# A two-layer hybrid trunk on one core: scan tables copied later and in two halves, and the first column tiles started after the last channel tile

## The chip, the cores and the metric

The kernel runs as one program on one core of a Trainium2 chip. The metric is device time in microseconds (us), from the start of the program to its end. The core has a matrix engine (PE, with its weight loads as PEld), a vector engine (DVE), a scalar engine (ACT), a general engine (POOL) and a sync engine (SP) that here only issues DMA transfers. They run at the same time, each through its own fixed list of instructions, and wait for each other through semaphores.

## What is computed

Two token groups (128 context tokens, 512 noisy tokens) go through the same two layers. Each layer, cut to what this case touches:

```python
sh1, sc1, g1, sh2, sc2, g2 = split(mod)          # mod = silu(c) @ w_ada + b_ada
u = x * (1.0 + sc1) + sh1                        # modulated input, D_MODEL = 1024
z = u @ p["w_in"]                                # the widest product: q, k, v, s_in, f_in, gates
ssm_y, ssm_state = _s5_bidirectional(s_in, ...)  # scan over time, both directions
ssm_y = gelu(ssm_y); ssm_y = ssm_y * sigmoid(ssm_y @ p["w_glu"] + p["b_glu"])
merged = g_a * (attn @ w_br_attn) + g_s * (ssm_y @ w_br_ssm) + g_f * (four @ w_br_four)
x = layer_norm(ALPHA * x + g1 * (merged @ p["w_out"]))
h = dwconv3((x * (1.0 + sc2) + sh2) @ p["w_up"]); ...; x = layer_norm(ALPHA * x + g2 * (... @ p["w_down"]))
```

The scan is a complex linear recurrence with per-state factors `lb` and input factors `f`. The kernel works it in blocks of eight time steps, for which it needs the powers of `lb` up to eight and `f` times those powers: these are the scan tables.

## The kernel before, in words

**Products.** Every large product is made in f32 out of three matmuls (L137 to L139): weights and activations are each split in a high part (`wh`, `uh`: a cast on ACT, L113) and a low part (`wl`, `ul`: what the cast lost, a subtraction on DVE, L115, or for some weights on POOL, L119). The weights of one column tile come by DMA as `wraw` (three buffers, issued by SP), are split, and serve both token halves: half 0 has 256 columns, half 1 has 384. `mm_wz` is the product with `w_in` (the code calls it wz).

**Start of layer 0.** `mod` is made in eight channel tiles dt = 0 to 7 (`ada_first`): a 1 MB block `ablk` arrives by DMA, is multiplied on PE (`adps`, L254), copied by ACT (`adar`, L257), transposed on PE (`adpt`, L259) and added up on DVE. After each channel tile `block(dt)` scales that part of x into `ut` (on ACT, L381, or on POOL, L379; two buffers for both halves) and splits it into `uh` and `ul`. Meanwhile the first four column tiles of half 0 are run piece by piece (`mm_first`, L1365): `WAT` says after which channel tile each begins. `MOD0` says which channel tiles are scaled on POOL. The operands of half 1 are made from dt = 5 on, between the others.

**Scan tables.** `ssm_scalars` makes the powers `PW` and the factors `FB` for both layers on DVE, in a scratch pool `zoh`. Eight copies on ACT, 64 x 512 elements each (L574 to L578), lay them out as `LT` and `FTab`.

**Preparation of the scan** (`ssm_prep`): eight chunks for layer 0, which DVE, DVE and POOL take in turn, later eight for layer 1, all on POOL. A chunk reads `bc` (by DMA, few buffers, so a load waits until PE has finished with an earlier chunk), multiplies it with `FTab` to `wbt` and with `LT` to `wct` (L647 to L649), and PE transposes `wbt` (`ptp`, copied by ACT to `wtt`) and multiplies `wct` (`pkp`). The results go to DRAM (`wbd`, `wcd`, `pd`) and come back as `wbs`, `wcs`, `Ms`. DVE begins with the preparation of layer 0 when the last operands are split. In the same stretch `shift` adds the position shift to x on DVE (L405), out of two PSUM banks that `mm_wz` then needs.

**The scan of layer 0** (`ssm`): SP loads `U` (eight transfers of short rows out of `sd`), PE multiplies `wbs` with `U` (`psv`, L691), DVE scans (L707, L710), copies the states to `Hr` (L724 to L727), and PE makes the output (`psy`, L738 and L740), which ends in `Yh`, goes through DRAM and returns as the operand `gh` of the product with `w_glu`. These steps lie between the column tiles of `mm_wz`.

**Order.** A scheduler lays out each engine's list from the dependencies when the kernel is built, with its own estimate of durations; `behind(x)` and `issue_after` only say what may not stand ahead of x. Memory of a closed pool is given to later tiles: a tile in the place of `zoh` waits until `zoh` has been read for the last time.

## Time and profile before

| | before |
|---|---|
| time, median of 3 runs (lowest to highest) | 2274.53 us (2269.32 to 2278.03) |
| the profiled execution's own time | 2270.7 us |
| its span | 2268.9 us |
| mean granted TensorE clock | 0.987 of full speed |
| PE busy | 2192.8 us, 97% of the span |
| DVE, ACT, POOL busy | 66%, 39%, 28% of the span |

The span is what the trace covers; the time holds 1.8 us more. A busy PE can still run at half speed: the granted clock of a stretch tells that, and 0.5 of it is 1.2 GHz, 1.0 is 2.4 GHz. Times below are counted from the start of the span. Almost all that the change moves lies between 25 and 395 us, up to the first matmul of `w_glu`.

### The profile page before, as it was taken

The numbers are of one execution on the slowest core, as the hardware profiler recorded it, in microseconds if no ns is written. First come the engines' busy times: TensorE is split into PE (matmuls) and PEld (weight loads), VectorE is DVE, ScalarE is ACT, GpSimd is POOL, SyncE is SP. The second block draws the span as 40 slices with busy tenths as digits, with TensorE's granted clock in tenths as the row PEclk, the third lists the DMA queues.
The fourth block names the chain that finished last, engine by engine and source line by source line (L and its number), as shares of the span: only waits on it lengthen the run. The fifth ranks groups of instructions, "written<-read, shape, count | busy, mean of one in ns | idle before, by whom it ended". The sixth has DMA issues, their size and how long they took to land.

```text
span 2268.9 us, 40864 instructions
## 1 busy us (share of the span) xinstructions
PE 2192.8 (97%) x15696; PEld 2106.3 (93%) x15696; DVE 1488.4 (66%) x3646; ACT 880.5 (39%) x1799; POOL 626.9 (28%) x795
## 2 busy tenths in 40 slices
PE   6899999998999999999999999999999999999997
PEld 4899989898799999999999999999779999999997
DVE  7956751556647788998974277457755766465475
ACT  5343323344633532431434322334553543242243
POOL 0339952006465300100136000001536620110103
PEclk9999989999999999999999999999999999999998
DMA  7886665625042135445536735642204122222221
GB/s 276 219 260 214 204 190 188 207 86 183 1 127 84 62 107 167 143 146 171 158 91 175 179 128 149 179 140 85 70 5 151 57 84 66 84 75 65 84 75 47
DMA packets 172645, 294.00 MB, mean 130 GB/s; under 512 B 48129, under 2 KB 114081, under 8 KB 171425
## 3 DMA queue, kind: packets, MB, share of 16 engines
q1 hardware_dynamic: 171584, 291.12, 41.8%
q8 instruction: 124, 2.03, 0.4%
q14 instruction: 73, 0.59, 0.1%
q10 hardware_dynamic: 864, 0.26, 0.1%
HBM read 241.57 MB, written 49.75 MB: 128 GB/s over the span
## 4 chain that ended last, share of the span: by engine, by line
PE 83%; DVE 7%; DMA 3%; ACT 2%; issue 1%; SPq 1%; POOL 1%; POOLq 0%; DVEq 0%; ACTq 0%
PE mm_w_up L138 8%; PE mm_w_up L137 8%; PE mm_w_up L139 8%; PE mm_wz L137 6%; PE mm_wz L138 6%; PE mm_wz L139 6%; PE mm_w_down L139 4%; PE mm_w_down L137 4%; PE mm_w_down L138 4%; PE mm_qkv L1114 4%; PE mm_pv L1179 2%; PE mm_w_br L137 2%; PE mm_w_br L138 2%; PE mm_w_br L139 2%; PE pt L1232 2%; PE S L1221 2%
## 5 line engine op out<-in xcount | busy, mean ns | idle before, releaser
L113 ACT CAST wh<-wraw 128x1024 fp32r<-128x1024 f32 (+1 forms) x224 | 232.8, 1040 | 446.5 <-PE mm_w_down L138 118.2
L138 PE MATMUL mm_w_up<-ul,wh 128*128 128x256 f32 (+1 forms) x1280 | 393.9, 309 | 0.0
L139 PE MATMUL mm_w_up<-uh,wl 128*128 128x256 f32 (+1 forms) x1280 | 393.8, 309 | 0.0
L137 PE MATMUL mm_w_up<-uh,wh 128*128 128x256 f32 (+1 forms) x1280 | 391.9, 309 | 0.4 <-ACT wh L113 0.4
L119 POOL TENSOR_TENSOR wl<-wraw,wh 128x256 fp32r<-128x256 f32 x224 | 175.2, 814 | 711.8 <-ACT wh L113 710.6
L115 DVE TENSOR_TENSOR wl<-wraw,wh 128x1024 fp32r<-128x1024 f32 (+1 forms) x168 | 211.7, 1260 | 160.6 <-ACT wh L113 159.1
L137 PE MATMUL mm_wz<-uh,wh 128*128 128x384 f32 (+1 forms) x832 | 266.2, 321 | 7.3 <-ACT uh L113 4.0
L1258 DVE SCALAR_TENSOR_TENSOR acc<-mm_w_up,cw,acc 128x127 f32<-128x127 f32 (+2 forms) x616 | 229.0, 399 | 60.0 <-ACT acc L1264 32.3
L138 PE MATMUL mm_wz<-ul,wh 128*128 128x384 f32 (+1 forms) x832 | 262.3, 315 | 0.4 <-POOL ul L119 0.3
L139 PE MATMUL mm_wz<-uh,wl 128*128 128x384 f32 (+1 forms) x832 | 262.1, 315 | 0.0
L137 PEld LDWEIGHTS mm_w_up<-uh,wh 128*128 128x128 f32 x1280 | 242.0, 189 | 0.6 <-ACT wh L113 0.6
L139 PEld LDWEIGHTS mm_w_up<-uh,wl 128*128 128x128 f32 x1280 | 242.3, 189 | 0.2 <-POOL wl L119 0.2
L138 PEld LDWEIGHTS mm_w_up<-ul,wh 128*128 128x128 f32 x1280 | 242.2, 189 | 0.0
L139 PE MATMUL mm_w_down<-hh,wl 128*128 128x256 f32 (+1 forms) x632 | 195.1, 310 | 0.6 <-DVE wl L115 0.6
L138 PE MATMUL mm_w_down<-hh,wh 128*128 128x384 f32 (+1 forms) x632 | 195.5, 310 | 0.0
L137 PE MATMUL mm_w_down<-hh,wh 128*128 128x384 f32 (+1 forms) x632 | 193.5, 311 | 0.0
L137 PEld LDWEIGHTS mm_wz<-uh,wh 128*128 128x128 f32 x832 | 160.2, 193 | 16.5 <-issue 6.1
L138 PEld LDWEIGHTS mm_wz<-ul,wh 128*128 128x128 f32 x832 | 159.9, 192 | 2.0 <-issue 1.0
L139 PEld LDWEIGHTS mm_wz<-uh,wl 128*128 128x128 f32 x832 | 159.7, 192 | 0.7 <-issue 0.4
L289 DVE SCALAR_TENSOR_TENSOR adjunk<-araw,cb 128x512 f32<-128x512 f32 x192 | 138.3, 720 | 16.9 <-DMA araw<-in_w_ada_t_dram 14.1
L1264 ACT ACTIVATE acc<-mm_w_up,cw 128x384 f32<-128x384 f32 (+1 forms) x176 | 107.8, 614 | 62.5 <-PE mm_w_up L139 62.3
L139 PEld LDWEIGHTS mm_w_down<-hh,wl 128*128 128x128 f32 x632 | 119.1, 189 | 1.5 <-DVE wl L115 1.5
(464 smaller groups left out, 5212.4 us busy)
## 6 DMA issues: line engine op xcount, KB each, us to landing
wraw<-in_w_up_dram SPq DMA_DIRECT2D x88, 512.0 KB, 3.5
wraw<-in_wz_dram SPq DMA_DIRECT2D x64, 512.0 KB, 4.1
araw<-in_w_ada_t_dram SPq DMA_DIRECT2D x48, 512.0 KB, 3.8
araw<-in_w_ada_dram SPq DMA_DIRECT2D x32, 512.0 KB, 3.9
wraw<-in_w_down_dram SPq DMA_DIRECT2D x32, 512.0 KB, 3.5
wraw<-in_w_br_dram SPq DMA_DIRECT2D x24, 512.0 KB, 3.8
td<-gt SPq DMA_DIRECT2D x48, 192.0 KB, 1.9
tl<-td SPq DMA_DIRECT2D x48, 192.0 KB, 3.5
```

Source lines behind the costliest of these rows:

```text
L113: nc.scalar.copy(h, src)
L115: return nc.vector.tensor_tensor(l, src, h.bitcast(F32), OP.subtract)
L119: last = eng.tensor_tensor(l[:, w], src[:, w], h[:, w].bitcast(F32), OP.subtract)
L137: mm(ps, wh, xh, start=j == 0, stop=False)
L138: mm(ps, wh, xl, start=False, stop=False)
L139: mm(ps, wl, xh, start=False, stop=j == n - 1)
L289: nc.vector.scalar_tensor_tensor(junk[:, :k.stop - k.start], raw[:, d], 1.0, cb[v], OP.mult, OP.mult, accum_out=part[:, c, vec - a, dt + d ...
L1114: nc.tensor.matmul(ps[:, :256], lt, w[:, c0:c0 + 256], start=k == 0, stop=k == 23)
L1179: nc.tensor.matmul(po[64 * hh:64 * hh + 64, :256], vt[:, kt + 1, kv * 64:kv * 64 + 64], PT[hh][:, kt], start=kt == 0, stop=kt == 5, tile_p ...
L1221: nc.tensor.matmul(S[:, b, :384], q, kt[:, hl, P + b * 384:P + (b + 1) * 384], start=hl == 0, stop=hl == 1)
L1258: nc.vector.scalar_tensor_tensor(o, src, w, o, OP.mult, OP.add)
L1264: nc.scalar.activation(acc, ps, AF.Identity, bias=b, scale=w1)
```

## The change

The numbers `WAT` and `MOD0` change, the table copies leave `ssm_scalars` for a function of their own, and the operands of half 1 are all made after the last channel tile.

- `WAT` goes from (3, 6, 7, 7) to (3, 7, 7, 7): the second column tile also begins only after the last channel tile.
- `MOD0`: half 1 was scaled for dt = 1, 3, 5, 7 on POOL and else on ACT; now all eight are on POOL.
- Half 1 is split only after channel tile 7 and its matmuls have been written.
- `ssm_tables(l)` copies the half of the tables that layer l reads, in eight copies of 64 x 256 elements, `FTab` first, and negates its part of `LT` on DVE. The copies for layer 0 stand behind the last cast of half 1, those for layer 1 behind the last `wtt` copy of the preparation of layer 0.
- The scratch pool `zoh` stays open until the second table copies and is closed there.

```diff
@@ -53,8 +53,8 @@
 ART = "wraw"
 WB = 3
 XB = 5
-WAT = (3, 6, 7, 7)
-MOD0 = (((), ()), ((1, 3, 5, 7), ()))
+WAT = (3, 7, 7, 7)
+MOD0 = (((), ()), (range(8), ()))
 FS = 10
 MODS = (((1, 3, 5, 7), ()), ((), (1, 3, 5, 7)))
 
@@ -110,7 +110,7 @@
 
     def split(self, h, l, src, eng=None):
         nc = self.nc
-        nc.scalar.copy(h, src)
+        self.cast = nc.scalar.copy(h, src)
         if eng is None:
             return nc.vector.tensor_tensor(l, src, h.bitcast(F32), OP.subtract)
         n = l.shape[-1]
@@ -474,7 +474,10 @@
         self.LT = p.tile([P, 3, G, 8], F32, name="LT")
         self.FT = p.tile([P, 2, G, 8], F32, name="FTab")
         L8 = self.L8 = s.tile([P, 2, G, 2], F32, name="L8")
-        with tc.tile_pool(name="zoh", bufs=1) as z:
+        self.zoh = ExitStack()
+        if True:
+            z = self.zoh.enter_context(tc.tile_pool(name="zoh", bufs=1))
+
             def t(n):
                 return z.tile([P, G], F32, name=n)
             V = nc.vector
@@ -567,22 +570,29 @@
             V.tensor_tensor(f[:, 1, 0], acc, den, OP.mult)
             a = [f[:, ri].broadcast_to((P, 8, G)) for ri in range(2)]
             cmul(FB, 0, 8, a, [PW[:, ri, 0:8] for ri in range(2)], 8)
-            fw, bw = slice(0, 64), slice(64, 128)
-            for ri in range(2):
-                o = self.LT[:, ri].rearrange("p g t -> p t g")
-                cp = nc.scalar.copy
-                cp(o[fw], PW[fw, ri, 1:9])
-                cp(o[bw, ::-1], PW[bw, ri, 1:9])
-                o = self.FT[:, ri].rearrange("p g t -> p t g")
-                cp(o[fw, ::-1], FB[fw, ri])
-                cp(o[bw], FB[bw, ri])
-            V.tensor_scalar(self.LT[:, 2], self.LT[:, 1], -1.0, None, op0=OP.mult)
             V.tensor_copy(L8[:, 0, :, 0], PW[:, 0, 8])
             V.tensor_copy(L8[:, 0, :, 1], PW[:, 1, 8])
             V.tensor_scalar(L8[:, 1, :, 0], PW[:, 1, 8], -1.0, None, op0=OP.mult)
             V.tensor_copy(L8[:, 1, :, 1], PW[:, 0, 8])
             self.fzero = p.tile([P, 2, G], F32, name="fzero")
             V.tensor_copy(self.fzero, f[:, :, 0])
+            self.powers = PW, FB
+
+    def ssm_tables(self, l):
+
+        PW, FB = self.powers
+        cp = self.nc.scalar.copy
+        gs = slice(32 * l, 32 * l + 32)
+        fw, bw = slice(0, 64), slice(64, 128)
+        for ri in range(2):
+            o = self.FT[:, ri, gs].rearrange("p g t -> p t g")
+            cp(o[fw, ::-1], FB[fw, ri, :, gs])
+            cp(o[bw], FB[bw, ri, :, gs])
+        for ri in range(2):
+            o = self.LT[:, ri, gs].rearrange("p g t -> p t g")
+            cp(o[fw], PW[fw, ri, 1:9, gs])
+            cp(o[bw, ::-1], PW[bw, ri, 1:9, gs])
+        self.nc.vector.tensor_scalar(self.LT[:, 2, gs], self.LT[:, 1, gs], -1.0, None, op0=OP.mult)
 
     def ssm_open(self):
 
@@ -658,7 +668,7 @@
                 pt = zp.tile([P, 512], F32, name="ptp", tag="ptp", bufs=1)
                 for q in range(4):
                     nc.tensor.transpose(pt[:, q * P:(q + 1) * P], w[:, 2 * hh + q // 2, q % 2], self.ident)
-                nc.scalar.copy(wt[:, 2 * hh:2 * hh + 2], pt.rearrange("p (g r q) -> p g r q", g=2, r=2))
+                self.turned = nc.scalar.copy(wt[:, 2 * hh:2 * hh + 2], pt.rearrange("p (g r q) -> p g r q", g=2, r=2))
             self.ld(wb[ch], wt.rearrange("p g r q -> p (g r q)"))
             c = z.tile([P, 4, 2, P], F32, name="wct", tag="wct", bufs=2)
             prod(c, 0, (lr, nb(cr)), (li, nb(ci)), OP.subtract)
@@ -1345,13 +1355,9 @@
 
         def block(dt):
             nc.vector.tensor_scalar(sc[:, dt], self.mod[0][:, 1, dt], 1.0, None, op0=OP.add)
-            for half in range(2):
-                if half == 0 or dt > XB:
-                    ends[half] = self.modsplit(xs[half][:, dt], half, sc, sh, dt, self.u[half, "h"], self.u[half, "l"])
+            ends[0] = self.modsplit(xs[0][:, dt], 0, sc, sh, dt, self.u[0, "h"], self.u[0, "l"])
             if dt == XB:
                 self.ld(xs[1], self.i["xt"][:, :, HS[1]])
-                for d in range(dt + 1):
-                    ends[1] = self.modsplit(xs[1][:, d], 1, sc, sh, d, self.u[1, "h"], self.u[1, "l"])
             while len(tiles) < 4 and (WAT[len(tiles)] == dt):
                 src = ("wz", (0, len(tiles)))
                 self.first[src] = self.wunit(self.usrc(src))
@@ -1364,17 +1370,25 @@
                     for k, (a, b) in enumerate(((h, "h"), (h, "l"), (l, "h"))):
                         nc.tensor.matmul(ps, a[:, w], self.u[0, b][:, kt], start=kt == 0 and k == 0, stop=kt == KT - 1 and k == 2)
                 t[1] = dt + 1
+            if dt == KT - 1:
+                for d in range(KT):
+                    ends[1] = self.modsplit(xs[1][:, d], 1, sc, sh, d, self.u[1, "h"], self.u[1, "l"])
 
         with tc.tile_pool(name="first", bufs=1, side="right") as fp, tc.tile_pool(name="firstp", bufs=1, space=PSUM) as self.adp:
             self.adar = fp.tile([P, 256], F32, name="adar")
             self.ablk[0] = self.ada_block(fp, 0)
             self.ld(xs[0], self.i["xt"][:, :, HS[0]])
             self.ada_first(fp, block)
+        with self.behind(self.cast):
+            self.ssm_tables(0)
         self.pin = False
         self.pre = {j: t[0] for j, t in enumerate(tiles)}
         self.xd = [self.dram.tile([P, KT, NTOK], F32, name=f"xd{l}") for l in range(NL)]
         with self.behind(ends[0]), self.behind(ends[1]):
             self.ssm_prep(0, (0, 0, 1))
+            with self.behind(self.turned):
+                self.ssm_tables(1)
+            self.zoh.close()
             self.shift(xs, self.xd[0])
         for l in range(layers):
             self.layer(l)
```

In the lists of the engines the change shows at three places. The names are those of the sections above; `x2` is two equal instructions in a row, and a number behind a name tells two tiles apart.

**ACT at the start, before:** the eight table copies stand between the scalings (`ut`) and casts (`uh_260` of half 0) of the last channel tiles and ahead of the second weight cast (`wh`).

```order
L574 COPY LT<-PW 64x8x64
L575 COPY LT<-PW 64x8x64
L113 CAST uh_260<-ut 128x256
L577 COPY FTab<-FB 64x8x64
L578 COPY FTab<-FB 64x8x64
L381 ACTIVATE ut<-xs,mod_85,su_264 128x128 x2
L381 ACTIVATE ut<-xs,mod_85,su_264 128x384
L113 CAST wh<-wraw 128x1024
L113 CAST uh_260<-ut 128x256
L577 COPY FTab<-FB 64x8x64
L578 COPY FTab<-FB 64x8x64
L113 CAST uh_262<-ut 128x384
```

The same place after: the last casts of half 0 (`uh_250`), then those of half 1 (`uh_252`), and only then the tables, half as long.

```order
L113 CAST wh<-wraw 128x1024
L381 ACTIVATE ut<-xs,mod_85,su_254 128x128 x2
L113 CAST uh_250<-ut 128x256
L113 CAST uh_252<-ut 128x384 x3
L792 COPY sre<-mm_first 128x256
L113 CAST uh_252<-ut 128x384
L792 COPY sre<-mm_first 128x256 x2
L113 CAST uh_252<-ut 128x384 x4
L589 COPY FTab<-FB 64x8x32
L590 COPY FTab<-FB 64x8x32
```

Nothing of the tables is left between the casts of half 0, and no scaling of half 1 is on ACT any more; they are eight in a row on POOL.

**SP around the loads of U, before:** `U` is loaded while the preparation of layer 0 is under way.

```order
L103 DMA Ms<-pd_695 16x8x128 x2
L103 DMA bc<-in_ssm_bc_dram 128x256
L103 DMA pd_695<-ksb 128x144
L103 DMA Ms<-pd_695 16x8x128 x4
L103 DMA U<-sd_1302 16x32x80 x2
L103 DMA wcd_694<-wct 128x1024
L103 DMA U<-sd_1302 16x32x80 x6
L103 DMA Ms<-pd_695 16x8x128
L103 DMA wbd_693<-wtt 128x1024
```

After, `U` stands behind the last chunk of that preparation, with all that belongs to it in one row; the first of them waits for an ACT instruction, since `U` lies where `zoh` lay.

```order
L103 DMA wbd_692<-wtt 128x1024
L103 DMA U<-sd_1311 16x32x80 x5
L103 DMA pd_694<-ksb 128x144
L103 DMA U<-sd_1311 16x32x80 x3
L103 DMA wbs<-wbd_692 128x1024 x2
L103 DMA Ms<-pd_694 16x8x128 x16
L103 DMA wcd_2195<-wct 128x1024
L103 DMA bc<-in_ssm_bc_dram 128x256
L103 DMA td_1313<-gt 128x384
L103 DMA td_1313<-gt 128x256
L103 DMA wbs<-wbd_692 128x1024
```

What moved: eight loads of `U`, two of `wbs` and sixteen of `Ms` now stand in a row, and behind them the `bc` of the second chunk of layer 1, which was ahead of the first chunk's `wcd` before, and the next `wbs`.

**POOL behind that, after:** the first chunk of layer 1 ends with `wct_2237`, the second begins with `bc_2268`.

```order
L658 TENSOR_TENSOR pb_2242<-bc_2197,LT_105 128x512
L659 TENSOR_TENSOR wct_2237<-wct_2237,pb_2238 128x4x128
L659 TENSOR_TENSOR wct_2237<-wct_2237,pb_2242 128x4x128
L641 TENSOR_TENSOR pt1_2276<-fzero_247,bc_2268 128x64
L642 TENSOR_TENSOR bb_2272<-fzero_247,bc_2268 128x64 x2
L657 TENSOR_TENSOR wbt_2285<-bc_2268,FTab_106 128x4x128
```

The `wcd_2195` of SP stores `wct_2237`, and the load of `bc_2268` stands behind it, so that POOL's second chunk now waits for SP, and SP for POOL's first.

On PE the first `psv` goes from row 456 of the list to row 876, the first `psy` that reads `Hr` from 1384 to 1634 and the last `psy` from 1534 to 1779. The first matmul of `w_glu` is row 1958 in both, and from there to the end the lists are the same but for a few swaps.

## Rows read from the trace of the kernel before

**Rows 1.** The page's chain that ended last: share of the span by engine.

```profile
PE 83%; DVE 7%; DMA 3%; ACT 2%; issue 1%; SPq 1%; POOL 1%; POOLq 0%; DVEq 0%; ACTq 0%
```

**Rows 2.** PE's waits, 0 to 60 us: total, times, longest, in us.

```profile
PE mm_first L1365 <- ACT uh L113: 6.7, 2, 5.5
```

**Rows 3.** Groups by line and form, ACT, 24 to 62 us: busy, mean ns | idle before.

```profile
L381 ACT ACTIVATE ut<-xs,mod,su 128x384 f32<-128x384 f32 x4 | 2.8, 699 | 0.1
L578 ACT COPY FTab<-FB 64x512 f32<-64x512 f32 x2 | 2.3, 1138 | 0.0
```

**Rows 4.** SP's timeline, then DMA issues of 15 to 27 us with us to landing.

```profile
25.73 0.90 SPq L103 DMA_DIRECT2D wraw<-in_wz_dram  x2
...
wraw<-in_wz_dram SPq DMA_DIRECT2D x3, 512.0 KB, 12.0
```

**Rows 5.** Busy us (instructions) of PE, PEld, DVE, ACT, POOL; granted clock; then PE's timeline.

```profile
40.00:43.00 3.00, 2.75 (x13) 2.46 (x13) 1.53 (x3) 2.96 (x5) 0.67 (x1) 0.50 0.46 115
46.60:50.20 3.60, 3.60 (x33) 3.60 (x31) 2.91 (x14) 1.92 (x6) 1.06 (x1) 1.00 0.71 204
...
55.62 0.45 PE L137 MATMUL mm_wz<-uh,wh 128*128 128x384 f32 x1 [0.30 <-ACT sre L782]
```

**Rows 6.** POOL's and DVE's timeline: start, duration, idle before and its releaser.

```profile
43.85 0.67 POOL L379 TENSOR_SCALAR ut<-xs,su,mod 128x384 f32<-128x384 f32 x1 [1.94 <-DVE ul L115]
48.49 1.06 POOL L379 TENSOR_SCALAR ut<-xs,su,mod 128x384 f32<-128x384 f32 x1 [3.98 <-DVE mod L263]
...
54.67 0.19 DVE L623 TENSOR_SCALAR nci<-bc 128x64 f32<-128x64 f32 x1
```

**Rows 7.** The position shift on DVE, and the PE matmul behind it.

```profile
82.22 6.44 DVE L405 TENSOR_TENSOR xs<-xs,mm_shift 128x256 f32<-128x256 f32 x16
...
85.00 0.58 PE L137 MATMUL mm_wz<-uh,wh 128*128 128x256 f32 x1 [1.27 <-DVE xs L405]
```

**Rows 8.** SP's loads of U, PE's first psv and wait, counts and clock behind it.

```profile
106.24 5.81 SPq L103 DMA_DIRECT2D U<-sd  x6
...
119.99 3.67 PE L691 MATMUL psv<-U,wbs 128*128 128x80 f32 x16 [2.81 <-DMA Ms<-pd]
...
122.00:126.00 4.00, 4.00 (x18) 3.90 (x18) 0.85 (x2) 1.94 (x9) 0.55 (x3) 0.51 1.07 398
130.00:270.00 140.00, 140.00 (x1196) 130.68 (x1193) 100.79 (x272) 54.10 (x132) 112.88 (x151) 1.00 0.66 217
```

**Rows 9.** SP's Ms loads; POOL's first chunk of layer 1 and the start of the second.

```profile
126.94 3.80 SPq L103 DMA_DIRECT2D Ms<-pd  x6
...
169.73 0.40 POOL L631 TENSOR_TENSOR pt<-fzero,bc 128x64 f32<-128x64 f32 x1 [4.19 <-DMA bc<-in_ssm_bc_dram]
...
175.70 2.51 POOL L649 TENSOR_TENSOR wbt<-wbt,pb 128x512 f32<-128x512 f32 x2
...
185.82 1.29 POOL L649 TENSOR_TENSOR wct<-wct,pb 128x512 f32<-128x512 f32 x1
```

**Rows 10.** The output of the scan: PE's timeline, DVE's copies, counts and clock.

```profile
277.96 0.67 PE L740 MATMUL psy<-Hr,wcs 128*128 128x80 f32 x4
...
324.80 0.61 PE L740 MATMUL psy<-Hr,wcs 128*128 128x80 f32 x4
...
294.18 1.51 DVE L727 COPY Hr<-Vst 64x512 f32<-64x512 f32 x1
...
299.25 0.62 DVE L727 COPY Hr<-Vst 64x512 f32<-64x512 f32 x1
...
280.00:296.00 16.00, 14.39 (x111) 13.44 (x111) 14.05 (x19) 3.35 (x10) 16.00 (x23) 0.91 0.79 211
...
317.00:325.00 8.00, 7.37 (x35) 7.40 (x36) 2.19 (x5) 1.52 (x4) 2.38 (x2) 0.57 0.24 92
```

**Rows 11.** The operand of w_glu on ACT, and PE's first matmul of w_glu.

```profile
341.04 4.07 ACT L799 CAST gh<-yb 128x256 fp32r<-128x256 f32 x6
...
394.56 0.33 PE L137 MATMUL mm_w_glu<-gh,wh 128*128 128x384 f32 x1
```

## The prediction

> **What bounds the kernel now.** The chain of waits comes first: 83% of the span is PE's own work [rows 1]. A gain is therefore worth only as much earlier as PE gets through its list, and what the change moves ahead of the first `w_glu` matmul at 394.56 us [rows 11] counts one for one, because the lists are the same behind it. So I then read PE's waits, and for each what the engine waited for had to wait for. There are four places. At the start PE waits 5.5 us in one piece for the cast `uh` [rows 2], and ACT, which makes it, is busy with table copies: each of the four groups like that of L578 holds two copies of 1.1 us [rows 3], 9 us in all. The wait has a second price: before 43 us PE issues 13 products in 3 us at clock 0.50, after 46.6 us 33 in 3.6 us at clock 1.00 [rows 5]. Second, `mm_wz` at 85.00 waits 1.27 us for the shift on DVE, whose sixteen pieces began at 82.22 [rows 7]. Third, the first `psv` waits 2.81 us for DMAs, and the clock falls to 0.51 behind it; from 130 to 270 us PE is full at clock 1.00 [rows 8]. Fourth, the output of the scan from 277.96 to 324.80 [rows 10].
>
> **The yardstick.** In 130 to 270 us PE has 1196 records in 140 us, 0.117 us each [rows 8]. The f32 matmuls of the lists (`psv`, `psy`, `ptp`, `pkp`) stand twice in the trace: the eight of the first two `psv` are sixteen records [rows 8]. Counting the lists so gives PE's own time between two places; it is an estimate, about 5% either way.
>
> **Start.** ACT loses 9 us of copies and four scalings, 2.8 us [rows 3]. What is then late next is the DMA: the weights of tiles two to four, issued at 25.73, take 12.0 us [rows 4], so they land at about 37.7 to 38.6. Three weight casts, the scalings and the casts of the last channel tile are then some 5 us of ACT work, to about 43. Three column tiles of 24 products remain, of which some 60 can run from 39 on, at first at 0.21 and then at 0.12 us each; I put their end at 49 (47.5 to 51), and the first `mm_wz` 6.3 us ahead of 55.62 [rows 5].
>
> Most of that is not kept. DVE begins the scan's preparation at 54.67 [rows 6], and it sets when the shift frees the bank at 85. The chain for half 1 now starts when half 0 is done, about 43: with two `ut` buffers, POOL's 0.67 to 1.06 us [rows 6], ACT's cast and DVE's subtraction (0.5 each) and the hand-overs give 2.3 us for a pair of buffers, 9.2 us for eight operands, end at 52.4. The first table copies follow on ACT at half of 1.14 [rows 3]; DVE's first product needs one pair of them and is held by about half a microsecond, while the rest hides behind DVE's first chunk. So DVE begins some 2.3 us earlier, and PE passes its place at 85.00 **2.5 us earlier** (0 to 6.3), at 82.5. Moving four scalings to POOL costs nothing there beyond this, as POOL was idle up to them; the four extra ones cover 0.7 us each on ACT.
>
> **From there to the end of the preparation.** PE's list from the shift to the last `ptp` of layer 0 is 420 products and 147 f32 matmuls, 714 records, 83 us; call its end T, about 165. `psv` no longer lies between, so PE asks for each chunk up to 13 us earlier than before, against a `bc` load that starts only when PE frees a buffer. DVE had free time there, so I take **0.5 us** (0 to 3).
>
> **The loads of U.** The old wait goes: 2.8 us, and the slow clock behind it, half of the some 6 us that PE worked at 0.51 to 0.64 [rows 8], 3 us: **-5.8**. What stands in its place is one queue. The second table copies end at T + 6 (last `wtt` copy, then eight of 0.56), and the first `U` waits for them, since it lies in `zoh`. Six loads of `U` took 5.81 us to issue [rows 8], so eight take 7.7, two `wbs` 0.9; six `Ms` took 3.80 [rows 9], so sixteen take 10. SP gets to `wcd` at T + 25, and behind it stands the `bc` of POOL's second chunk. The PE list from the last `ptp` to the first `psv` is 92 products and 36 f32 matmuls, 19 us; `U`, last issued at T + 14, needs about 8 us more (the wait before ended 8 us after the last issue): T + 21. A first wait of 1 to 2 us, with bounds 0 and 6.
>
> The second wait is the larger. POOL's first chunk (169.73 to 187.1, 17.4 us, 8.5 of them to the end of `wbt` [rows 9]) is ready in time, at T + 20. The `bc` behind SP's row lands at T + 29: 25.5 plus the 4 us for which POOL waited in the row at 169.73 [rows 9]. The first half of `wbt` follows 6.6 us later, T + 36. PE's list reaches that `ptp` at T + 29 to T + 31. That is 5 us (0 to 12). The `wbs` and the next weights stand behind the same `bc` and land within that wait. Two waits some 12 us apart cost the clock again, 3 us each at most; I take 4. Sum of this place: **+11** (1 to 24).
>
> **The output of the scan.** Between 277.96 and 324.80 the list holds 327 records, 38 us, and took 47. DVE copies `Hr` there, 1.51 us while POOL is busy, 0.62 when POOL rests; at the end the clock is 0.57 [rows 10]. After the change these rows come some 28 us later behind the end of `psv`, DVE is through with its scan, and POOL is further on in its own list. I take **-4** (-9 to 0). The Trainium skill, page "SBUF — State Buffer", section "Who interferes with whom", says that DVE copies can claim the port pair shared with GpSimd for a whole instruction, and that the other blocks. The two durations agree with it.
>
> The cover at the end gets thin: from the last `psy` to `w_glu` PE had 70 us, now 173 products and 16 f32 matmuls, 24 to 29. The way through DRAM took from 324.8 to 345.1, where the casts `gh` end [rows 11], 20.3 us. It is hidden, with 4 to 9 us left.
>
> **Sum.** -2.5 + 0.5 - 5.8 + 11 - 4 = -0.8 us. The profiled execution (2270.7, span 2268.9) would go to about 2270; it lies 3.8 under the median of the runs, 2274.5, so the forecast is **2274 us**.
>
> **Rivals.**
> 1. *SP's row costs nothing.* For it: PE was full for 140 us with POOL behind it [rows 8], so small delays were covered before. Against it: `bc` stands directly behind `wcd`, which needs POOL's previous chunk. Then the 11 become 1: -10.8, **2264**; if the start also keeps its 6.3, 2260.
> 2. *Slower: SP's row takes the pace of U.* One mechanism at one place: if `Ms` issues at U's 0.97 us instead of 0.63, SP reaches `bc` 5.5 us later, POOL's chunks, which then follow one another without a gap, all come later, and POOL is busy again under the output of the scan, so the 4 us there are not won. -2.5 + 0.5 - 5.8 + 19 + 0 = +11, **2286**. It decides from the point where `bc` lands later than T + 33.
> 3. *The change does not reach PE at the start.* POOL's eight scalings stand against DVE's subtractions: 1.06 us instead of 0.67 in the row at 48.49, where DVE worked too [rows 6]. At 0.4 us more for each operand, 3 us, DVE begins no earlier than 54.67 and the 2.5 are gone: **2277**. The same section of the Trainium skill speaks for this: a DVE instruction with two SBUF inputs contends with a GpSimd instruction that reads SBUF. The rows at 43.85 and 48.49 show both cases, and by the rule all eight would be slow.
>
> **How the numbers follow.** Forecast 0.55, rival 1 0.2, rival 2 0.13, rival 3 0.12. The range takes rival 1 to its middle and rival 2 nearly to its end: 2262 to 2287. A measurement of this kernel can tell about 0.5%, 11.4 us, from no change. Faster by that is under 2263.2: half of rival 1 and a little of the forecast, 0.15. Slower is over 2285.9: half of rival 2 and a little of the rest, 0.12. The rest, 0.73, is within.
>
> **What would show it.** Right: no table copy between the casts of half 0, the first `mm_wz` near 49, but the one behind the shift only 2 to 3 us earlier than 85; the first `psv` near 185 with a short wait; a POOL gap of some microseconds before the second chunk of layer 1, named by `bc`, and PE waiting for that chunk's `wbt` near 195; the output of the scan under 45 us; `w_glu` within 4 us of 394.6. Wrong: no wait between 180 and 200 (rival 1), POOL waiting past T + 33 (rival 2), or DVE beginning the preparation at 54 or later (rival 3). A wait for `gh` ahead of `w_glu` would mean that the thin cover failed, which no term above holds.

## The result, and the profile after

| | before | after |
|---|---|---|
| time, median (lowest to highest), us | 2273.24 (2269.32 to 2278.03) | 2299.8 (2297.81 to 2303.82) |
| ratio, 95% interval | | 1.0123 (1.0099 to 1.0147) |
| span of the profiled execution, us | 2268.9 | 2299.5 |
| mean granted TensorE clock | 0.987 | 0.979 |
| first `psv` of layer 0, us | 119.99 | 187.85 |
| first `w_glu` matmul, us | 394.56 | 418.3 |

The kernel became 1.2% slower, 26.6 us by the medians. The prediction, 2274 with a range of 2262 to 2287, was wrong, and the time lies outside the range. Of the 30.6 us by which the spans differ, 23.7 are there at the first `w_glu` matmul.

The start first. PE's timeline of the changed kernel (start, duration, matmul, idle before and what ended it) answers to [rows 5] and [rows 7]; under it are two windows with busy us (instructions) of PE, PEld, DVE, ACT and POOL and the granted clock, one of the kernel before and one of the changed kernel.

```profile
48.39 0.34 PE L137 MATMUL mm_wz<-uh,wh 128*128 128x384 f32 x1
...
58.52 0.69 PE L137 MATMUL mm_wz<-uh,wh 128*128 128x384 f32 x1 [5.58 <-ACT sre L792]
...
82.47 0.58 PE L137 MATMUL mm_wz<-uh,wh 128*128 128x256 f32 x1 [2.33 <-DVE xs L405]
```

```profile
0.00:85.00 85.00, 56.80 (x540) 46.89 (x540) 69.80 (x253) 40.67 (x77) 12.99 (x24) 0.94 0.72 245
```

```profile
0.00:82.47 82.47, 54.95 (x510) 46.47 (x510) 67.52 (x251) 35.16 (x72) 14.46 (x26) 0.93 0.70 241
```

Both places came as forecast: 48.39 (49) and 82.47 (82.5). But ahead of the second one PE had got through 540 matmuls before, and through 510 now. The 30 that are missing are `pkp` of the preparation, 64 of them then and 34 now; they stand behind that place in the new list. In between PE stood still for 5.58 us: the copy `sre` that it waited for comes on ACT at 58.00, behind the eight table copies (51.59 to 57.02) and a weight cast. In the kernel before, no wait of PE between 53 and 77 us lasts over 0.8 us.

The row on SP that carries `U`, `wbs` and `Ms`, and POOL behind it (for [rows 8] and [rows 9]):

```profile
172.38 2.44 SPq L103 DMA_DIRECT2D U<-sd  x5
175.69 0.34 SPq L103 DMA_DIRECT2D pd<-ksb  x1
176.07 2.84 SPq L103 DMA_DIRECT2D U<-sd  x3
178.96 1.88 SPq L103 DMA_DIRECT2D wbs<-wbd  x2
180.88 13.65 SPq L103 DMA_DIRECT2D Ms<-pd  x16
194.96 0.34 SPq L103 DMA_DIRECT2D wcd<-wct  x1
195.40 0.37 SPq L103 DMA_DIRECT2D bc<-in_ssm_bc_dram  x1
```

```profile
198.51 0.29 POOL L641 TENSOR_TENSOR pt<-fzero,bc 128x64 f32<-128x64 f32 x1 [15.46 <-DMA bc<-in_ssm_bc_dram]
```

PE's two long waits of that stretch, from its timeline, and a window over both in the columns of the windows above:

```profile
187.85 3.67 PE L701 MATMUL psv<-U,wbs 128*128 128x80 f32 x16 [3.30 <-DMA wbs<-wbd]
...
202.93 2.10 PE L701 MATMUL psv<-U,wbs 128*128 128x80 f32 x16 [3.17 <-DMA wbs<-wbd]
```

```profile
184.00:208.00 24.00, 15.61 (x108) 14.50 (x107) 3.28 (x8) 6.56 (x22) 9.49 (x15) 0.79 0.93 260
```

SP issues nothing else from 172.38 to 195; POOL, which had waited 4.19 us for its `bc` in [rows 9], stands still for 15.46. PE loses 8.4 us of 24 to idling, and the mean clock of this window is 0.79.

The trace also shows what SP waited for. Fifteen of its sixteen `Ms` take 0.30 to 0.43 us each; the rest of the 13.65 us is one of 1.55 and the gaps between them. Eight of them in a row, from 182.21 to 189.73, begin 0.02 us after an earlier transfer has landed: `U` lands at 185.25 and 186.61, and an `Ms` begins at 185.27 and 186.63. Each of these eight begins with seven other transfers of SP still under way, and in the whole run none begins with more. So the row went at the pace at which `U` and `wbs` landed.

Then the output of the scan (for [rows 10]): DVE's copies, PE's wait, POOL's list at the same time, and windows over this wait and the next.

```profile
326.23 11.48 DVE L735 COPY Hr<-Vst 64x512 f32<-64x512 f32 x1
337.73 0.63 DVE L737 COPY Hr<-Vst 64x512 f32<-64x512 f32 x1
...
338.41 1.14 PE L750 MATMUL psy<-Hr,wcs 128*128 128x80 f32 x4 [7.67 <-DVE Hr L737]
```

```profile
326.04 0.27 POOL L633 TENSOR_SCALAR nci<-bc 128x64 f32<-128x64 f32 x1
326.25 0.25 POOL L687 TENSOR_TENSOR ksb<-ksb,dd 128x16 f32<-128x16 f32 x1
326.43 2.10 POOL L657 TENSOR_TENSOR wct<-bc,LT 128x512 f32<-128x512 f32 x2
328.46 1.31 POOL L659 TENSOR_TENSOR wbt<-wbt,pb 128x512 f32<-128x512 f32 x1
329.71 0.35 POOL L643 TENSOR_TENSOR bb<-pt,bb 128x64 f32<-128x64 f32 x1
329.99 1.08 POOL L658 TENSOR_TENSOR pb<-bc,LT 128x512 f32<-128x512 f32 x1
331.00 2.79 POOL L119 TENSOR_TENSOR wl<-wraw,wh 128x256 fp32r<-128x256 f32 x4
333.73 1.08 POOL L658 TENSOR_TENSOR pb<-bc,LT 128x512 f32<-128x512 f32 x1
334.74 2.51 POOL L659 TENSOR_TENSOR wct<-wct,pb 128x512 f32<-128x512 f32 x2
```

```profile
326.00:350.00 24.00, 16.33 (x81) 15.58 (x81) 18.23 (x18) 3.41 (x8) 11.25 (x15) 0.67 0.24 66
372.00:388.00 16.00, 12.76 (x64) 12.54 (x62) 6.15 (x12) 2.11 (x5) 3.02 (x4) 0.60 0.51 179
```

A copy that takes 0.6 us with POOL at rest, and 1.5 us beside a busy POOL in [rows 10], lasted 11.48. POOL worked through all of it without a gap, and the copy ended 0.46 us after POOL's last instruction, which ends at 337.25. PE waited 7.67 us; the clock stood at half from 334.4 to 351.4 us. A second, smaller wait (3.24 us for a DMA, up to 376.39) cost the clock once more, the last window.

**The account.** For the experiments the same count is made of every kernel: what PE lost up to its first `w_glu` matmul, by stretch. In windows of 2 us, the loss is the idle time plus the busy time multiplied by one minus the granted clock. The rest, time less loss, should be the same in all kernels, since the list is; it is 338 to 346 us, so the count closes to some 4 us. The last column is the ratio of the times. The stretches are those of the one execution that was profiled, the ratio is that of the medians, and the two can lie apart: the profiled execution of the kernel before with `Hr` on ACT took 2273.39 us, 7.9 over its median, that of the start alone with both mends 2256.75, 9.2 under it, the others lie within 5.5.

| kernel | 0–100 | 100–160 | 160–240 | 240 to `w_glu` | rest | `w_glu` at | ratio to before |
|---|---|---|---|---|---|---|---|
| before | 33.5 | 5.8 | 0 | 11.8 | 343.5 | 394.6 | 1 |
| after | 35.4 | 0 | 15.8 | 24.9 | 342.3 | 418.3 | 1.0123 |
| start alone | 34.9 | 11.1 | 0 | 6.9 | 341.8 | 394.7 | 1.0013 |
| all but the late second tables | 38.5 | 11.6 | 0 | 10.0 | 339.1 | 399.2 | 1.0027 |
| late second tables alone | 31.1 | 0 | 10.9 | 8.5 | 345.5 | 396.0 | 1.0017 |
| after, `Hr` copied on ACT | 35.8 | 0 | 21.5 | 6.3 | 341.6 | 405.2 | 1.0031 |
| after, `Hr` as a maximum on DVE | 35.0 | 0.4 | 17.6 | 15.4 | 339.9 | 408.3 | 1.0066 |
| after, three `bc` | 34.5 | 0 | 12.3 | 2.6 | 340.2 | 389.6 | 1.0012 |
| after, three `bc`, `Hr` on ACT | 37.1 | 0 | 11.8 | 8.6 | 338.2 | 395.7 | 1.0031 |
| before, `Hr` on ACT | 32.9 | 7.1 | 6.6 | 1.7 | 343.8 | 392.0 | 0.9977 |
| before, three `bc` | 35.0 | 0 | 0.1 | 5.9 | 344.0 | 385.0 | 0.998 |
| start alone, three `bc` | 34.7 | 5.7 | 0.1 | 6.5 | 340.5 | 387.5 | 0.9977 |
| before, three `bc`, `Hr` on ACT | 34.9 | 0 | 0 | 1.3 | 344.0 | 380.2 | 0.9951 |
| start alone, three `bc`, `Hr` on ACT | 36.5 | 2.6 | 0 | 2.8 | 339.8 | 381.7 | 0.9965 |

Behind `w_glu` the changed kernel loses 6.8 us more. Most of it is the same kind of event in layer 1: a `psy` waits 1.60 us for `Ms`, and a window over it, of the changed kernel, shows the clock at 0.68. The kernel before waits 1.24 us at the same `psy`, and its clock stays at 1.00 in the 16 us behind it.

```profile
1452.93 0.42 PE L748 MATMUL psy<-U,Ms 128*128 128x80 f32 x2 [1.60 <-DMA Ms<-pd]
```

```profile
1450.00:1466.00 16.00, 14.40 (x80) 14.23 (x80) 3.82 (x10) 3.72 (x8) 0.00 (x0) 0.68 0.31 109
```

16 us at 0.68 are some 5 us of PE's work lost. Why this `Ms` comes later was not looked into.

### The profile page after: what moved, and what is told of

The parts are those of the page before. It is cut to its first block, busy times and chain, and to the rows that moved or that the text cites. A ratio compares the mean times of both kernels' runs of the same rounds, so it can differ in the third digit from the quotient of the medians.

```text
span 2299.5 us, 40873 instructions
## 1 busy us (share of the span) xinstructions
PE 2209.4 (96%) x15696; PEld 2121.8 (92%) x15696; DVE 1482.4 (64%) x3647; ACT 883.3 (38%) x1803; POOL 622.6 (27%) x799
## 4 chain that ended last, share of the span: by engine, by line
PE 83%; DMA 3%; DVE 2%; POOL 1%; SPq 1%; issue 1%; ACT 1%; POOLq 0%; DVEq 0%; ACTq 0%
PE mm_w_up L138 9%; PE mm_w_up L137 9%; PE mm_w_up L139 9%; PE mm_wz L137 5%; PE mm_wz L138 5%; PE mm_wz L139 5%; PE mm_w_down L137 5%; PE mm_w_down L138 5%; PE mm_w_down L139 5%; PE mm_qkv L1124 4%; PE mm_pv L1189 2%; PE pt L1242 2%; PE S L1231 2%; PE mm_w_br L137 2%; PE mm_w_br L138 2%; PE mm_w_br L139 2%
## 5 line engine op out<-in xcount | busy, mean ns | idle before, releaser
L137 PE MATMUL mm_w_up<-uh,wh 128*128 128x256 f32 (+1 forms) x1280 | 391.9, 309 | 0.4 <-ACT wh L113 0.4
L137 PE MATMUL mm_wz<-uh,wh 128*128 128x384 f32 (+1 forms) x832 | 268.1, 323 | 14.4 <-ACT sre L792 5.6
L137 PEld LDWEIGHTS mm_w_up<-uh,wh 128*128 128x128 f32 x1280 | 242.0, 189 | 0.6 <-ACT wh L113 0.6
L137 PE MATMUL mm_w_down<-hh,wh 128*128 128x384 f32 (+1 forms) x632 | 193.5, 311 | 0.0
L137 PEld LDWEIGHTS mm_wz<-uh,wh 128*128 128x128 f32 x832 | 162.6, 196 | 22.4 <-issue 6.3
```

The costliest lines, as they stand in the source:

```text
L137: mm(ps, wh, xh, start=j == 0, stop=False)
```

## Experiments

### The parts alone

The changed kernel, with the second layer's tables copied at the start too, right behind the first:

```diff
         with self.behind(self.cast):
             self.ssm_tables(0)
+            self.ssm_tables(1)
+        self.zoh.close()
...
-            with self.behind(self.turned):
-                self.ssm_tables(1)
-            self.zoh.close()
```

> Both layers' tables are copied behind the last cast of half 1 and zoh is closed there; WAT, MOD0 and the later half 1 stay as in the changed kernel. Theory A (the loss comes from the second table copies: they keep zoh open, so U, wbs and Ms stand late and in one row on SP, and all that follows from it): nearly the whole loss of 27 us goes, and about 2.5 us of the start stay, less some 3 us for eight more copies ahead of the first chunk: 2270 to 2276 us, first psv near 120 us, no wait of POOL for bc over 6 us, no Hr copy over 2 us. Theory B (the new order of the start does it, for instance POOL's scalings or the later column tiles): 2290 us or more.

Measured: 2279.71 us, 1.0027 (1.0009 to 1.0045). PE's timeline of this kernel shows the next `mm_wz` unit waiting for `sre`, which stands behind sixteen table copies on ACT instead of eight, for 10.89 us, where the changed kernel waits 5.58:

```profile
63.50 0.69 PE L137 MATMUL mm_wz<-uh,wh 128*128 128x384 f32 x1 [10.89 <-ACT sre L792]
```

No `Hr` copy lasts over 1.69 us, and the 160 to 240 stretch is free of loss. So most of the 26.6 us needs the late second tables; the time is some 4 us over the range of theory A, and far under theory B.

The start alone: `WAT`, `MOD0` and half 1 behind the last channel tile, while the tables are copied where and as they were before.

```diff
-WAT = (3, 6, 7, 7)
-MOD0 = (((), ()), ((1, 3, 5, 7), ()))
+WAT = (3, 7, 7, 7)
+MOD0 = (((), ()), (range(8), ()))
...
+            if dt == KT - 1:
+                for d in range(KT):
+                    ends[1] = self.modsplit(xs[1][:, d], 1, sc, sh, d, self.u[1, "h"], self.u[1, "l"])
```

> Only WAT, MOD0 and the later half 1 of the change; the tables are copied as in the kernel before, in eight whole copies as soon as the powers are there. Theory A: the loss is not here, 2268 to 2276 us, first psv near 118 us. Theory B: 2290 us or more. Beside e1 this also prices the move of the first tables: if ACT's 9 us of copies at the start were what delayed the casts, the first mm_wz comes later here than the 48.4 us of the changed kernel, by 3 to 7 us.

Measured: 2277.22 us, 1.0013 (0.9993 to 1.0033). The first `mm_wz` runs at 53.79 instead of 55.62, and `w_glu` at 394.7, where it was. Delaying half 1 without moving the tables is worth nothing that can be measured. Here PE waits only 1.34 us for `sre` (at 59.46), but the old wait for `uh` is back, 5.46 us at 34.69, where the changed kernel waits 2.49: the two places of the tables on ACT cost PE a wait of the same size.

The late second tables alone: the kernel before, where only the half of the tables that layer 1 reads is copied behind the preparation of layer 0; the other half is copied at the old place, in eight copies of half the size.

```diff
+            self.powers = PW, FB
+            self.ssm_tables(0)
...
+            with self.behind(self.turned):
+                self.ssm_tables(1)
+            self.zoh.close()
```

> The kernel before, and of the change only the second layer's tables behind the preparation of layer 0, so that U, wbs and 16 Ms stand in one row on SP. Theory: this part alone carries the loss: 2294 to 2302 us, with SP's row about 25 us, a bc wait of POOL over 10 us, a wait of two psv of 3 us each and a DVE instruction held for 6 us or more in the output of the scan. Rival (the loss needs the start as well): 2274 to 2284, w_glu under 402.

Measured: 2277.23 us, 1.0017 (0.9997 to 1.0037): the theory fell and the rival held. SP's row and POOL's wait, in their timelines, are about as long as in the changed kernel:

```profile
172.49 12.91 SPq L103 DMA_DIRECT2D Ms<-pd  x16
```

```profile
190.87 0.29 POOL L642 TENSOR_TENSOR pt<-fzero,bc 128x64 f32<-128x64 f32 x1 [16.25 <-DMA bc<-in_ssm_bc_dram]
```

But the `psv` wait 1.8 and 0.5 us instead of 3.3 and 3.2, and no `Hr` copy lasts over 1.74 us. (A subtraction on DVE, at 226.22, is held for 6.23 us.) A wait of 16 us on POOL is therefore not in itself what costs PE its time. The two halves cost 0.27% and 0.17% by themselves, 0.44% together; the change costs 1.23%. Some 18 us come only from both together, with an uncertainty of some 8 us by the three intervals.

### What the two together do: the held copy

The changed kernel, with the `Hr` copies of layer 0 on ACT:

```diff
-                nc.vector.tensor_copy(Hc[fw, :16], V[fw, VP:VP + 16, gr])
-                nc.vector.tensor_copy(Hc[fw, 16:], V[fw, 0:64, gr])
+                cp = nc.scalar.copy if l == 0 else nc.vector.tensor_copy
+                cp(Hc[fw, :16], V[fw, VP:VP + 16, gr])
+                cp(Hc[fw, 16:], V[fw, 0:64, gr])
...
```

> The changed kernel with the four Hr copies of each chunk of layer 0 on ACT instead of DVE. In the changed kernel one such copy lies on DVE from 326.2 to 337.7 us, 11.5 us instead of 0.6, just as long as POOL runs without a gap, and PE waits 7.7 us for it and then runs 14 us at clock 0.5. Theory A, its last link (POOL's unbroken run blocks a DVE copy): no copy over 1.5 us here, the wait of 7.7 us and about 6 us of slow clock go: 2284 to 2290 us. Rival (the copy is long because its input is late, or the trace draws it so): ACT's copies or the psy behind them wait just as long, 2296 to 2302 us.

Measured: 2282.1 us, 1.0031 (1.0013 to 1.0049), some 18 us under the changed kernel, 2 us under the range of theory A, and near the 0.44% of the two halves. The longer copies take 1.05 to 1.11 us each on ACT, none is held, and PE is full in the window where it had waited:

```profile
320.00:350.00 30.00, 30.00 (x253) 28.42 (x251) 8.82 (x30) 19.73 (x33) 21.32 (x27) 1.00 0.72 201
```

POOL still waits 16.27 us for `bc` in this kernel, so what the copy on ACT gives back does not come from SP's row. It isn't purely the held copy either: the kernel before gains 0.23% by the same edit (below), some 5 us. And DVE is still held in this kernel, elsewhere: a subtraction for `wl` lasts 9.71 us from 208.19 on, and PE waits 3.77 us for it, which is in the 21.5 of the table.

The same copies stay on DVE, as an instruction with two inputs (the maximum of a value and itself):

```diff
+                def cp(o, x):
+                    return nc.vector.tensor_tensor(o, x, x, OP.max) if l == 0 else nc.vector.tensor_copy(o, x)
```

> The changed kernel with each Hr copy of layer 0 made on DVE as max(x, x), an operation with two inputs, instead of a copy with one; everything else as in the changed kernel, POOL's unbroken run too. Theory (it is the kind of DVE instruction: a copy gets no turn while POOL's instructions follow each other, one with two inputs does, as the scan's 0.3 us instructions at 325 us did): no such instruction over 3 us, PE's wait of 7.7 us goes: 2283 to 2291 us, like the run with the copies on ACT. Rival (DVE as a whole, or anything that reads the states, waits for POOL or for the scan): one of them lasts 8 us or more again, 2296 to 2302 us.

Measured: 2287.02 us, 1.0066 (1.0042 to 1.0089). The first of them is held for 11.54 us; in DVE's timeline it stands with the three behind it in one row, and PE waits as long as in the changed kernel:

```profile
326.51 14.65 DVE L735 TENSOR_TENSOR Hr<-Vst 64x512 f32<-64x512 f32 x4
...
339.13 1.14 PE L752 MATMUL psy<-Hr,wcs 128*128 128x80 f32 x4 [7.76 <-DVE Hr L735]
```

So it is not the copy as a kind of instruction: the theory's reason fell, though the time lies in its range. Of the 12.8 us that this kernel is faster than the changed one, most lie behind the held instruction: the wait of 3.24 us at 376 and its slow clock are missing, 8.3 us by the window above.

The changed kernel with a third buffer for `bc`, which takes POOL's wait away and lets POOL get on with its list:

```diff
-            bc = z.tile([P, 4, 4, 16], F32, name="bc", tag="bc", bufs=2)
+            bc = z.tile([P, 4, 4, 16], F32, name="bc", tag="bc", bufs=3)
```

> The changed kernel with three buffers for bc instead of two, so that the bc of POOL's second chunk of layer 1 is loaded ahead of the late loads of U; U, wbs and Ms stay late and in a row. Theory A, its middle link (SP's row delays POOL by 15.5 us, and that pushes POOL's run onto the Hr copies): POOL's wait of 15.5 us falls under 3, the Hr copy stays under 2 us, the waits at psv stay (3 us each): 2280 to 2290 us. Rival C (POOL is late because its first chunk waits for the second tables, whatever SP does): the copy is blocked all the same, 2296 us or more.

Measured: 2275.63 us, 1.0012 (0.9992 to 1.0032). POOL waits 3.05 us instead of 15.46, no `Hr` copy lasts over 1.41, and the stretch from 240 on loses 2.6 us instead of 24.9. Theory A's middle link holds and rival C falls; the time is some 4 us under the theory's range. The first two `psv` still wait 4.0 and 1.9 us: the first wait does not hang on POOL, the second at most in part. What is left for them is `U` and `wbs`, which SP issues only when the second table copies are done; that is read from the order, and no run moved `U` alone. `w_glu` comes 4.9 us earlier than in the kernel before, and layer 1 gives this back (its last `w_glu` matmul of L137 stands at 1483.7, before at 1480.6): a `psy` waits 1.95 us, and 10 us of slow clock begin at 1427.2.

That POOL's unbroken run is what holds the copy is read from the times, and from this kernel, where POOL's list comes earlier and no `Hr` copy is held. No run stopped POOL beside the same copy.

### What the mends are worth without the change

Three `bc` buffers and `Hr` on ACT help the kernel before as well, so the change has to be priced against that. All edits are those shown above. The kernel before with `Hr` on ACT, and with three `bc`:

> The kernel before with the four Hr copies of each chunk of layer 0 on ACT. There a copy took 1.5 us beside POOL and 0.6 alone, and the output of the scan lost 9 us to waits and slow clock. If DVE's slowed copies are what it lost them to, that stretch falls from 47 to 40 us and the kernel to 2264 to 2270 us; if not, it stays within 3 us of the kernel before.

> The kernel before with the third bc buffer. If the buffer repairs only what the change broke (SP's row ahead of the second chunk of layer 1), nothing is to be had here, since PE never waited for POOL's chunks: within 3 us of the kernel before. If the buffer itself is worth the 24 us that it gave to the changed kernel, this is 2255 us or less.

Measured: 2265.47 us, 0.9977 (0.9959 to 0.9995), and 2266.14 us, 0.998 (0.9961 to 0.9999). The gain of the buffer, 5.8 us, is more than was expected if it only repaired the change, and far from the 24 us of the other case. With `Hr` on ACT the output of the scan takes 35 us instead of 47. But DVE is held in this kernel too, at another place: a subtraction that makes `wl` (a row of DVE's timeline), with POOL at work without a gap from 209.9 to 222.1.

```profile
212.20 11.00 DVE L115 TENSOR_TENSOR wl<-wraw,wh 128x1024 fp32r<-128x1024 f32 x1 [1.61 <-ACT wh L113]
```

It costs PE 6.6 us there (160 to 240 in the table). This execution was the slowest of ten; whether the subtraction is held in the others is not known. With three `bc` the old wait of the first `psv` is gone (5.8 to 0). The start alone with three `bc`:

> The new order of the start (WAT, MOD0, half 1 last) with the tables copied as before, and the third bc buffer. By theory A no stretch has a blocked copy; the start gives 0 to 2.5 us: 2268 to 2275 us. If the late tables were worth something that the start alone does not give (first mm_wz at 48 instead of 54 us), this is slower than the changed kernel with three buffers by 2 to 4 us.

Measured: 2268.32 us, 0.9977 (0.9958 to 0.9997), as the kernel before with three `bc`: again nothing from the start. It is also 7 us faster than the changed kernel with three `bc`, so the 2 to 4 us that late tables were to be worth in the other case did not come.

Both mends together, in the kernel before, in the start alone and in the changed kernel:

> The kernel before with three buffers for bc and layer 0's Hr copies on ACT. Each alone gave 5.8 and 6.5 us. Theory (they mend two places that do not touch): 2258 to 2264 us, w_glu at 382 to 386, psy phase of layer 0 at 35 us or less. Rival (what they save at w_glu is given back behind it, as some of it was with bc alone): 2264 to 2270, though w_glu comes 9 us earlier.

> The start of the change alone (operands of half 1 last, second column tile late, tables as before), with bc in three buffers and Hr on ACT. If the start by itself is worth nothing, as the run of the start alone showed: the same as the kernel before with both mends, within 4 us. If the start's earlier first mm_wz was only lost to the other two places: 3 to 6 us under it.

> The changed kernel with both mends, three bc buffers and Hr on ACT. Theory (the change's loss is the place of the loads of U and the output of the scan; both mended, only the waits of the first psv for wbs, 5 to 9 us, are left): 5 to 10 us over the kernel before with both mends, 2265 to 2273. Rival (with the causes gone the earlier start shows): equal to it or up to 3 us less.

Measured: 2260.53 us, 0.9951 (0.9935 to 0.9967); 2265.95 us, 0.9965 (0.9946 to 0.9985); 2278.28 us, 1.0031 (1.0012 to 1.005). In the kernel before the two gains add (5.8 and 6.5 us alone, 13.8 together), and this version is faster than both kernels. The start with both mends is 5.4 us slower than that, a little outside the 4 us expected. Windows of the kernel before with both mends show PE nearly full where its two old losses were:

```profile
100.00:180.00 80.00, 80.00 (x714) 75.49 (x712) 55.96 (x107) 34.36 (x98) 49.29 (x66) 1.00 0.94 273
250.00:320.00 70.00, 68.72 (x582) 64.83 (x582) 26.85 (x70) 42.86 (x78) 50.97 (x67) 1.00 0.77 216
```

The change on top of the mends costs 17.8 us by the medians, more than the 5 to 10 that were expected. The two profiled executions lie 12.5 us apart; in them 11.8 us of loss lie at the first `psv`, as in the other kernels with late tables, and some 7 at one further wait behind it (the smaller rest of the table takes 6 back), a row of PE's timeline with the window after it:

```profile
358.39 0.42 PE L749 MATMUL psy<-U,Ms 128*128 128x80 f32 x2 [3.44 <-DMA td<-gt]
```

```profile
360.00:364.00 4.00, 4.00 (x20) 4.00 (x20) 0.45 (x2) 0.44 (x1) 0.00 (x0) 0.50 0.63 222
```

Again PE waits 3.4 us for a transfer and works at half clock behind it.

Subtracting like from like, the change costs 1.2% in the bare kernel, 0.5% where both versions have `Hr` on ACT, 0.3% where both have three `bc`, and 0.8% where both have both. Each of the last three is uncertain by some 0.3%, so their order is open, and none is a gain.

## Why the prediction was wrong, step by step

By the table and the spans, the sum of -0.8 us missed by 4.4 us at the start, 4.8 at the loads of U, 17.1 at the output of the scan and 6.8 behind `w_glu`; the smaller terms take 1.7 back, which makes the 30.6.

**Start, -2.5: the places were right, the gain was not there.** PE did pass the shift 2.5 us earlier, but with 30 `pkp` fewer behind it, some 3.5 us of PE's work at the yardstick of 0.117 us. What took the time is a wait that the sum put at nothing: of the first table copies it said that all but the first pair hide behind DVE's first chunk, and PE waited 5.58 us for the `sre` that ACT makes behind them. So two steps failed: that one, and the sentence that a place reached earlier counts one for one: this holds only where the same list stands ahead of the place, as at `w_glu`, and not at the shift. By the losses up to 100 us the start costs 1.9 us, and the start alone moved `w_glu` by 0.1 us. Of rival 3 (the gain is lost), the size came true, not the mechanism: DVE began the preparation at 52.19, as forecast, and of POOL's eight scalings four took 0.66 to 0.67 us, with no subtraction of DVE under way when they began.

**The old wait of `psv`, -5.8: right.** The stretch from 100 to 160 loses 5.8 us before and none after.

**The loads of U, +11: 15.8.** The parts were named rightly, and the size is inside the bounds of 1 to 24. Sixteen `Ms` took 13.65 us, not 10: 0.85 us each, between the two prices of [rows 8] and [rows 9]. The price of [rows 9] did not carry over, since there SP had no gap over 0.09 us between them, and here it waited for `U` and `wbs` to land. POOL's `bc` landed at 198.44; the last `ptp` of the preparation ends at 166.1, so that is T + 32, where T + 29 was put and T + 33 was rival 2's point. `U` landed at 186.61, where T + 21 was put. The wait of 5 us was put at POOL's chunk; PE waited instead twice for `wbs`, 3.3 and 3.2 us, and the run with three `bc`, where they are 4.0 and 1.9, shows that the first does not hang on `bc`, and the second at most in part.

**The output of the scan, -4: +13.1. This is the step that failed worst.** It reasoned that POOL would be further on in its list and DVE done with its scan. It gave POOL's work beside the copies a price of at most 0.9 us a copy, from rows in which the two alternated, and set the bounds at -9 to 0. The trace of before shows no held copy, but neither did it exclude one: a loss belonged in the bounds. In the late tables alone, without a held copy, the term comes out near the forecast, -3.3. The mended kernels leave its sign open, since the mends help the kernel before as well: against the kernel before with the same mend it is +4.6 with `Hr` on ACT, -3.3 with three `bc` and +7.3 with both. The whole second half of the sum holds for the late tables alone: forecast -5.8 + 11 - 4 = +1.2, measured -5.8 + 10.9 - 3.3 = +1.8, `w_glu` 1.5 us later.

**Rival 2** named the right direction and the right place (POOL busy again under the output of the scan) and priced it at 4 us not won, where 17 were lost against the term. (Its 19 for the place of the row is 2.5 more than the 11 and the 5.5 that it names.) Its name for the mechanism, SP's row at the pace of `U`, is what the landings show, although `bc` stayed just short of its T + 33. SP's row set where POOL's unbroken run fell; why the run then held the `Hr` copy, and in the late tables alone, with the same wait for `bc`, did not, is open.

**The thin cover** before `w_glu` was not what failed: PE goes from its last `psy` at 386.7 to `w_glu` at 418.3 with no wait over 0.8 us, 31.6 us for what was put at 24 to 29.

**Layer 1** was taken as unchanged, since the lists are nearly the same. Behind `w_glu` 6.8 us were lost, most of them to a wait of 1.60 us instead of 1.24 and the slow clock behind it. That can go either way: from the first to the last `w_glu`, the kernels here need between 1084 and 1094 us.

On the Trainium skill, page "SBUF — State Buffer", section "Who interferes with whom": it says that the engine that comes second to the port pair shared by DVE and GpSimd (POOL here) blocks fully, until the first has finished. The trace agrees that DVE can block, and that an instruction with two SBUF inputs does so like a copy (11.54 us beside 11.48). It differs in the length: the copy was held not for one POOL instruction, but over a run of them, the longest of which are 1.3 us each. That the port pair is what held it is not shown by any run.

## What to carry over

A place in the timeline that is reached earlier is a gain only if the same work has been done by then: count the matmuls ahead of it, or PE's idle time and clock loss, as in the table. A short wait of PE cost two to four times its length here where the clock fell behind it (2.81 us cost 5.8, 3.24 cost 8.3, 1.60 cost some 6), so two waits of 3 us, or one wait moved to a place with no cover, undo what several microseconds of earlier start bring. Where one engine's list is shifted against another's, a forecast from rows of their old meeting is weak: here the same copy took 0.6, 1.5 and 11.5 us, and what removed this hold was to give the copy to ACT, or to take away the wait that had shifted POOL's list. Neither removed every hold: a subtraction on DVE was still held in both kernels (9.71 and 5.67 us). And a mend that helps the kernel before as well must be priced there too, before its gain is put down to the change.

## What was not expected of the hardware

DVE instructions with SBUF inputs were held for over 4 us, across several POOL instructions, in eight of the fourteen kernels: 11.48 us (`Hr` copy), 11.54 (maximum), and ten subtractions for `wl` of 4.06 to 11.00 us, where the longest DVE instruction of the kernel before takes 3.38. Ten of these twelve ended 0.5 to 1.1 us after the end of POOL's unbroken run, about the time that such an instruction takes beside an idle POOL (0.6 us for the copy, 0.9 to 1.2 for the subtraction). In the other two (6.23 us in the late tables alone, 4.06 in the run with the maximum) POOL had no gap, and DVE came through while a small POOL instruction took 1.27 or 1.28 us instead of 0.23 to 0.29. In between, in the same kernels, DVE and POOL took turns, and the longer copies lasted 0.6 to 1.7 us beside a busy POOL. DVE's scan instructions, which have one operand in PSUM, took 0.20 to 0.30 us throughout. What decides between taking turns and holding was not found and was not tried by itself: it stays open.

A row of transfers on SP can be slow although each is quick to issue. Sixteen loads of 64 KB took SP 12.9 to 14.6 us in the six kernels with late second tables, 0.81 to 0.91 us each, though most of them take 0.30 to 0.44 by themselves; in each of these kernels several begin 0.02 us after an earlier transfer has landed, with seven still under way. In the whole runs of the kernel before and the changed kernel, no transfer of SP begins with more than seven of its others under way.
